# Attention's v product with seven block products in seven of sixteen units, and the probabilities' block moves at once over two queues

## Chip, cores and metric

The kernel runs on one core of a Trainium2 chip. The metric is the device time of one execution in microseconds; three runs of the kernel before gave 2028.94, 2030.40 and 2030.67 us, median 2030.40.

## What is computed

A two-layer decoder trunk in float32, 256 tokens of 2048 features: layer 0 mixes by causal pooling, layer 1 by attention with shared keys and values, and each has a gated convolutional feed-forward part after it. The part that matters here is layer 1's attention, 16 heads of 128 features:

```
k_shared = (h @ shared_w_k).reshape(B_, S, N_HEADS, HEAD_DIM)
v_shared = (h @ shared_w_v).reshape(B_, S, N_HEADS, HEAD_DIM)
...
q = (h @ w_q).reshape(B_, S, N_HEADS, HEAD_DIM)
for window, dil in DILATED_BRANCHES:
    o, lse = _dilated_branch(q, k, v, window, dil)
...
o = jnp.sum(wts[..., None] * jnp.stack(outs, axis=0), axis=0)
return o.reshape(B_, S, D_MODEL).astype(h.dtype) @ w_o
```

The three branches read the same scores with different masks, so the kernel merges them into one set of probabilities a head: exp of the masked scores, weighted by how many branches see a key.

## The kernel before

The program is a list of **units**. A unit is one 512x512 block of a weight (1 MB), its load, its split, its matmuls and, for the last block of a group, a `post` that takes the sums from PSUM. Float32 accuracy comes from splitting each weight and each activation in a high and a low part and adding three products. PE runs the units in the order of the list; `run_units` (from L130) does this for each unit i:

- `ahead(i)` (L111) issues loads up to five units ahead from SP's queue (L72) into three `raw` buffers, and splits up to three units ahead: ACT casts the high part (L82), DVE subtracts for the low part (L83), into four `wh` and four `wl` buffers;
- then the unit's matmuls on PE;
- then whatever was put off with `later(n, fn)` and is due now, n units after it was put off; then `post`.

An engine runs its instructions in the order in which this program writes them. So what `later` writes stands on DVE behind splits for units up to three further on, and a transfer on SP stands behind the loads written before it and ahead of those written after.

`group` (L165, L166: 16 pairs of a 128x512 and a 128x256 matmul) makes the feature-major products K, q and o-proj, with four PSUM accumulators of 128 features; `group_tm` (L238 to L240: 24 matmuls of 128x512) makes the token-major ones, such as v, with two. `group_tm` can also take units as **seven products**: the block is cut in 2x2, combinations of the quarters are made, and seven block products replace eight (L227 to L229, 42 matmuls of 128x256). Such a unit becomes two, "a" (18 matmuls, 3 products) and "b" (24, 4 products, no load of its own); its splits are `split_sums` (L89 to L109): for "a" ACT casts twice (L103) and DVE does L104, L106 twice, L107, L109; for "b" ACT casts twice (L96) and DVE subtracts twice (L97). The `raw` buffer of the block is free only when "b" is split. In the kernel before the feed-forward parts use this and attention doesn't.

Attention runs over four quarters hq of the output columns, four heads each: K(hq), q(hq), v(hq), four units each, then o-proj. For a quarter, put off from the end of q:

- `scores` for two heads at a time: PE L988, L989 into PSUM; DVE L994 to L1011 and ACT L1001 make probabilities, two heads in one tile `p`;
- `blocks` for quarters 0 to 2: DVE transposes 32x32 blocks within `p` (L1034) into a buffer `pb`, and 16 DMAs of 32 partitions by 6 runs of 128 bytes (L1043) put each block where the full transpose has it, tile `pTs`; all 16 on SP, eight after one unit and eight after two;
- `transposes` for quarter 3 instead: PE transposes, three a head (L1026), ACT copies;
- `outputs` for two heads: PE L1056, L1057 multiply by v (`vt`, from `v_post`, L952), ACT casts (L1058) and DVE subtracts (L1059) into `o`, which o-proj reads.

One buffer of its pool is left for `pb`, so the DVE transpose of a quarter's second pair of heads waits for all 16 moves of the first.

Of the kernel before, what the change touches and what calls it, by code (L numbers as in the profile page):

```python
# [9 lines left out]
F32 = mybir.dt.float32  # L10
F32R = mybir.dt.float32r
I32 = mybir.dt.int32
AF = mybir.ActivationFunctionType
OP = mybir.AluOpType
# [3 lines left out]
T = 256  # L18
P = 128
# [13 lines left out]
def trunk(ctx: ExitStack, tc: tile.TileContext, x, pool_w_in, pool_w_grp, pool_scale, pool_w_out,  # L33
          attn_w_q, attn_w_o, shared_w_k, shared_w_v, ffn_w_up, ffn_conv_w, ffn_conv_b, ffn_w_down,
          ln1_g, ln1_b, ln2_g, ln2_b, out):
    nc = tc.nc
    V, A, PE = nc.vector, nc.scalar, nc.tensor
# [7 lines left out]
    lnp = ctx.enter_context(tc.tile_pool(name="lnp", bufs=1))  # L45
    psp = ctx.enter_context(tc.tile_pool(name="psp", bufs=8, space=bass.MemoryType.PSUM))

    def bank(nm):
        return psp.tile([P, 512], F32, name=nm, tag="ps")
# [70 lines left out]
    def later(n, fn):  # L120
        if n == 0:
            fn()
        else:
            pending.append([n, fn])
# [52 lines left out]
    def group(w, r0s, c0, ncol, xqs, post, mode="ab", mids=(), shifted=False):  # L177
        ps = []
        for j, (r0, nr) in enumerate(r0s):
            last = j == len(r0s) - 1  # L180
            units.append((w[r0:r0 + nr, c0:c0 + ncol],
                          mm_quad(xqs[j], ps, j == 0, last, mode, mids[j] if j < len(mids) else None, shifted),
                          (lambda: post(ps)) if last else None))
# [98 lines left out]
    def quad_tile(nm):  # L282
        return xcp.tile([P, 4, 2, XW], F32R, name=nm, tag="xc")

    def lo_part(dst, src, n):
        V.tensor_tensor(dst[:, 0:n, 1, :T], src, dst[:, 0:n, 0, :T].bitcast(F32), OP.subtract)

    def split_act(dst, src):
        n = src.shape[1]
        A.copy(dst[:, 0:n, 0, :T], src)  # L290
        lo_part(dst, src, n)

    rows4 = [(512 * j, 512) for j in range(4)]

    pools = {}
    H, XC, XP, ST = {}, {}, {}, {}
    vec, cvec, gbx = [], [], {}
    ident = const.tile([P, P], F32, name="ident")
# [8 lines left out]
    xsrcs = [lambda j=j: XC[j] for j in range(4)]  # L307
# [150 lines left out]
    def add_last(w, rows, srcs, first, lay, which, after=None):  # L458
        for c in range(4):
            group(w, rows, 512 * c, 512, srcs, resid_last(c, first, lay, which, after),  # L460
                  mode="a" if c == 3 else "ab", shifted=c > 0 and not first)
# [481 lines left out]
    scale = 1.0 / math.sqrt(P)  # L943
    qk, pr, oq, pT, vts = {}, {}, {}, {}, {}

    def v_post(c):
        def post(t, ps):
            if t == 0:
                vts[c] = pools["attn"].tile([P, 2, 512], F32, name="vt", tag="vt")
                A.copy(vts[c][:, 0, :], ps)  # L950
            else:
                V.tensor_copy(vts[c][:, 1, :], ps)  # L952
                if c == 3:
                    later(1, lambda: transposes(c, (0, 1)))
                    later(2, lambda: transposes(c, (2, 3)))
                later(2 if c == 3 else 4, lambda: outputs(c, (0, 1)))
                later(3 if c == 3 else 7, lambda: outputs(c, (2, 3)))
        return post

    def qk_post(nm, hq):  # L960
        def post(ps):
            later(2 if hq == 0 and nm == "k" else 0, lambda: evac(ps))

        def evac(ps):
            ap = pools["attn"]
            o = ap.tile([P, 4, T], F32, name=nm, tag=nm)
            qk[nm] = o

            if hq == 0 and nm == "k":
                norm_evac(ps, 4, lambda m: o[:, m, :])  # L970
            else:
                for m in range(4):
                    A.copy(o[:, m, :], ps[m][:, T:])
                    V.tensor_tensor(o[:, m, :], o[:, m, :], ps[m][:, :T], OP.add)
            if nm == "q":
                later(2, lambda: scores(hq, range(0, 2)))
                later(3, lambda: scores(hq, range(2, 4)))
                if hq < 3:
                    later(4, lambda: blocks(hq, (0, 1)))
                    later(7, lambda: blocks(hq, (2, 3)))  # L980
        return post

    def scores(hq, ms):
        ap = pools["attn"]
        for m in ms:
            ps = bank("s")
            q, k = qk["q"][:, m, :], qk["k"][:, m, :]
            PE.matmul(ps[:, 0:P], q[:, :P], k[:, :P], start=True, stop=True)  # L988
            PE.matmul(ps[:, P:3 * P], q[:, P:], k, start=True, stop=True)  # L989
            if m % 2 == 0:  # L990
                two = ap.tile([P, 2, 3, P], F32, name="p", tag="p", bufs=2)
            s = two[:, m % 2]
            sf, nf, cf = (t.rearrange("p a b -> p (a b)") for t in (s, negm, cnt))
            V.scalar_tensor_tensor(sf, ps[:, :3 * P], scale, nf, op0=OP.mult, op1=OP.add)  # L994
            mx = ap.tile([P, 6], F32, name="mx", tag="mx", bufs=4)
            parts = ((0, slice(0, P)), (1, slice(P, 3 * P)))
            for t, sl in parts:
                V.tensor_reduce(mx[:, t:t + 1], sf[:, sl], AX.X, OP.max)
            V.tensor_scalar(mx[:, 2:4], mx[:, 0:2], -1.0, None, op0=OP.mult)
            for t, sl in parts:  # L1000
                A.activation(sf[:, sl], sf[:, sl], AF.Exp, bias=mx[:, 2 + t:3 + t])  # L1001
            pr[hq, m] = (s, mx, two)
        for m in ms:
            s, mx, _ = pr[hq, m]
            sf, cf = (t.rearrange("p a b -> p (a b)") for t in (s, cnt))
            for t, sl in parts:
                V.scalar_tensor_tensor(sf[:, sl], sf[:, sl], 1.0, cf[:, sl], op0=OP.mult, op1=OP.mult,
                                       accum_out=mx[:, 4 + t:5 + t])
            V.reciprocal(mx[:, 0:2], mx[:, 4:6])
            for t, sl in parts:  # L1010
                V.tensor_scalar(sf[:, sl], sf[:, sl], mx[:, t:t + 1], None, op0=OP.mult)  # L1011

    def turned(hq, ms):
        pool, tag = (pools["attn"], "pT") if ms[0] == 0 else (lnp, "sq")
        t = pool.tile([P, 2, 3 * P], F32, name="pTs", tag=tag)
        for m in ms:
            pT[hq, m] = t[:, m % 2]
        return t

    def transposes(hq, ms):  # L1020
        t = turned(hq, ms)
        for m in ms:
            ps = bank("pT")
            s = pr.pop((hq, m))[0]
            for i in range(3):
                PE.transpose(ps[:, i * P:(i + 1) * P], s[:, i, :], ident)  # L1026
            A.copy(t[:, m % 2], ps[:, :3 * P])


    def blocks(hq, ms):  # L1030
        two = pr.pop((hq, ms[0]))[2]
        pr.pop((hq, ms[1]))
        b = hp.tile([P, 6 * P], F32, name="pb", tag="h")
        V.transpose(b, two.rearrange("p h s k -> p (h s k)"))  # L1034

        t = turned(hq, ms)
        to = t.rearrange("p h s -> p (h s)").rearrange("p (k a j) -> p a k j", k=6, a=4)
        fr = b.rearrange("p (k b j) -> p b k j", k=6, b=4)

        def move(rows):  # L1040
            for i in rows:
                for j in range(4):
                    nc.sync.dma_start(to[32 * j:32 * j + 32, i], fr[32 * i:32 * i + 32, j])  # L1043

        later(1, lambda: move((0, 1)))
        later(2, lambda: move((2, 3)))

    def outputs(hq, ms):
        if ms[0] == 0:
            oq[hq] = quad_tile("o")  # L1050
        vt = vts[hq]
        for m in ms:
            hd = slice(m * P, (m + 1) * P)
            ps = bank("o")
            t = pT.pop((hq, m))
            PE.matmul(ps[:, :T], vt[:, 0, hd], t[:, :T], start=True, stop=False)  # L1056
            PE.matmul(ps[:, P:T], vt[:, 1, hd], t[:, T:], start=False, stop=True)  # L1057
            A.copy(oq[hq][:, m, 0, :T], ps[:, :T])  # L1058
            V.tensor_tensor(oq[hq][:, m, 1, :T], ps[:, :T], oq[hq][:, m, 0, :T].bitcast(F32), OP.subtract)  # L1059

    for hq in range(4):
        x0 = hq == 0
        group(shared_w_k, rows4, 512 * hq, 512, psrcs if x0 else xsrcs, qk_post("k", hq), mode="x" if x0 else "ab")
        group(attn_w_q[0], rows4, 512 * hq, 512, xsrcs, qk_post("q", hq))
        group_tm(shared_w_v, rows4, 512 * hq, 512, xsrcs, v_post(hq))
    add_last(attn_w_o[0], rows4, [lambda j=j: oq[j] for j in range(4)], True, 1, 0, after=to_tokens)
    marks.append(len(units))
    ffn(1)
# [141 lines left out]
```

## Time and profile before

| | before |
|---|---|
| median of three runs | 2030.40 us |
| profiled execution, its own time | 2030.49 us |
| its span in the profile | 2028.6 us |
| PE busy | 2021.7 us (100%), 12496 matmuls |
| DVE busy | 1674.5 us (83%) |
| ACT busy | 1257.2 us (62%) |
| POOL busy | 75.0 us (4%) |
| attention, start of K(0) to start of o-proj | 934.7 to 1218.3 us |

How to read what follows: a timeline row is start, duration, engine, line, operation, output<-inputs, shapes and count, and in brackets the idle time just before it with what ended it. A duration includes what overlaps with the next instruction of the engine, so the cost of a matmul or a DVE operation in a row of them is the distance between two starts. A group row has busy time and mean duration in nanoseconds. A DMA row ends with the median from issue to landing.

### The profile page before, as it was taken

Reading aid. Unit: us, or ns where it says so; the run is one execution under the profiler, and the core shown is the slowest. Engines: PE = TensorE matmul, PEld = TensorE weight load, DVE = VectorE, ACT = ScalarE, POOL = GpSimd, SP = SyncE. Lnnn points to the kernel's source line nnn. Section 1 sums busy time; section 2 is a strip of 40 time slices with the busy share of each in tenths; the row PEclk is TensorE's granted clock in tenths of the full one; section 3 lists DMA queues with packets and bytes.
Section 4 is the critical chain, followed back from the end, with each engine's and each line's share of the span. In section 5 each row is a group of like instructions: output and inputs, shape, how many; then the busy total and the mean of one; then the engine's idle time right before and its main releaser. Section 6 shows DMA issues by size and latency. Waiting matters only on the chain.

```text
span 2028.6 us, 31127 instructions
## 1 busy us (share of the span) xinstructions
PE 2021.7 (100%) x12496; PEld 1809.4 (89%) x12496; DVE 1674.5 (83%) x1998; ACT 1257.2 (62%) x1685; POOL 75.0 (4%) x111
## 2 busy tenths in 40 slices
PE   9999999999999999999999999999999999999999
PEld 8898988899889988889888888998899989989987
DVE  6859887899789999879756657787889888989898
ACT  5544686667766676657533444577667676667672
POOL 2000000000000001100000000000000000100100
PEclk9999999999999999999999999999999999999999
DMA  8565467666655757864566554557666756666665
GB/s 257 201 206 188 165 209 210 190 192 225 210 191 187 234 188 219 232 226 165 191 197 195 169 185 168 187 178 216 187 198 197 228 187 213 198 213 196 209 214 180
DMA packets 278305, 405.92 MB, mean 200 GB/s; under 512 B 80414, under 2 KB 95668, under 8 KB 277904
## 3 DMA queue, kind: packets, MB, share of 16 engines
q1 hardware_dynamic: 266144, 389.72, 57.9%
q0 software_dynamic: 11584, 13.55, 4.4%
q8 instruction: 98, 1.61, 0.3%
q10 hardware_dynamic: 432, 0.66, 0.1%
q14 instruction: 47, 0.39, 0.1%
HBM read 380.01 MB, written 2.10 MB: 188 GB/s over the span
## 4 chain that ended last, share of the span: by engine, by line
PE 99%; DMA 0%; SPq 0%; DVE 0%; ACT 0%; issue 0%; DVEq 0%
PE acc L165 43%; PE acc L166 22%; PE t L238 3%; PE t L239 3%; PE t L240 3%; PE acc L169 3%; PE acc L170 3%; PE acc L168 3%; PE s L228 3%; PE s L229 3%; PE s L227 3%; PE t L228 2%; PE t L227 2%; PE t L229 2%; PE s L989 0%; PE o L1056 0%
## 5 line engine op out<-in xcount | busy, mean ns | idle before, releaser
L165 PE MATMUL acc<-xc,wh 128*128 128x512 f32 x3264 | 1151.9, 396 | 0.0
L166 PE MATMUL acc<-xc,wl 128*128 128x256 f32 x3264 | 916.3, 281 | 0.0
L83 DVE TENSOR_TENSOR wl<-raw,wh 128x2048 fp32r<-128x2048 f32 (+2 forms) x320 | 692.4, 2168 | 248.4 <-ACT wh L82 243.9
L165 PEld LDWEIGHTS acc<-xc,wh 128*128 128x128 f32 x3264 | 616.0, 189 | 143.7 <-DVE o L1059 0.6
L82 ACT CAST wh<-raw 128x2048 fp32r<-128x2048 f32 (+2 forms) x320 | 578.1, 1812 | 225.7 <-PE acc L165 118.3
L166 PEld LDWEIGHTS acc<-xc,wl 128*128 128x128 f32 x3264 | 615.5, 189 | 0.5
L96 ACT CAST wh<-raw 128x1024 fp32r<-128x1024 f32 x112 | 117.4, 1053 | 150.2 <-DVE raw L107 134.1
L97 DVE TENSOR_TENSOR wl<-raw,wh 128x1024 fp32r<-128x1024 f32 x112 | 133.8, 1221 | 0.5 <-ACT wh L96 0.5
L103 ACT CAST wh<-raw 128x1024 fp32r<-128x1024 f32 x112 | 87.7, 832 | 41.2 <-PE acc L165 24.7
L106 DVE TENSOR_TENSOR wl<-raw,wh 128x1024 fp32r<-128x1024 f32 x112 | 101.9, 951 | 1.3 <-ACT wh L103 0.9
L586 ACT ACTIVATE c<-u,cv 128x256 f32<-128x256 f32 x172 | 89.5, 593 | 19.4 <-DVE f L649 8.2
L228 PE MATMUL t<-wl,g 128*128 128x256 f32 x328 | 92.2, 281 | 0.0
L227 PE MATMUL t<-wh,g 128*128 128x256 f32 x328 | 92.1, 281 | 0.0
L229 PE MATMUL t<-wh,g 128*128 128x256 f32 x328 | 91.9, 280 | 0.0
L271 POOL DMA_DIRECT2D ht<-w x24 | 20.3, 847 | 1808.1 <-ACT wh L103 1060.1
L577 ACT COPY u<-acc 128x256 f32<-128x256 f32 x164 | 54.0, 372 | 46.9 <-PE acc L166 46.8
L229 PE MATMUL s<-wh,xs 128*128 128x256 f32 x296 | 82.6, 279 | 0.0
L228 PE MATMUL s<-wl,xs 128*128 128x256 f32 x296 | 82.6, 279 | 0.0
L227 PE MATMUL s<-wh,xs 128*128 128x256 f32 x296 | 82.5, 279 | 0.0
L591 ACT ACTIVATE a<-u,cv 128x256 f32<-128x256 f32 x172 | 73.6, 500 | 12.3 <-DVE g L659 6.5
L591 ACT ACTIVATE u<-u,cv 128x256 f32<-128x256 f32 x172 | 73.5, 500 | 0.0
L109 DVE TENSOR_TENSOR raw<-raw 128x1024 f32<-128x1024 f32 x56 | 68.6, 1225 | 1.9
(279 smaller groups left out, 3444.8 us busy)
## 6 DMA issues: line engine op xcount, KB each, us to landing
raw<-in_ffn_w_up_dram SPq DMA_DIRECT2D x160, 1024.0 KB, 4.9
raw<-in_ffn_w_down_dram SPq DMA_DIRECT2D x80, 1024.0 KB, 5.1
raw<-in_pool_w_out_dram SPq DMA_DIRECT2D x16, 1024.0 KB, 5.0
raw<-in_shared_w_k_dram SPq DMA_DIRECT2D x16, 1024.0 KB, 5.1
raw<-in_attn_w_q_dram SPq DMA_DIRECT2D x16, 1024.0 KB, 5.3
raw<-in_shared_w_v_dram SPq DMA_DIRECT2D x16, 1024.0 KB, 5.9
raw<-in_attn_w_o_dram SPq DMA_DIRECT2D x16, 1024.0 KB, 5.0
raw<-in_pool_w_in_dram SPq DMA_DIRECT2D x12, 1024.0 KB, 5.6
```

Source lines behind the costliest of these rows:

```text
L82: A.copy(wh[i][:, s], r[:, s])
L83: V.tensor_tensor(wl[i][:, s], r[:, s], wh[i][:, s].bitcast(F32), OP.subtract)
L96: A.copy(h[:, :, n], r[:, :, n])
L97: V.tensor_tensor(l[:, :, n], r[:, :, n], h[:, :, n].bitcast(F32), OP.subtract)
L106: V.tensor_tensor(l[:, k, n], r[:, k, n], h[:, k, n].bitcast(F32), OP.subtract)
L165: PE.matmul(ps[m], h[:, k, c], q[:, k, :, :T], start=st, stop=False)
L166: PE.matmul(ps[m][:, :T], l[:, k, c], q[:, k, 0, :T], start=False, stop=sp and not shifted)
L227: PE.matmul(to, xh, h[:, k, n], start=opens and kk == 0, stop=False)
L228: PE.matmul(to, xh, l[:, k, n], start=False, stop=False)
L229: PE.matmul(to, xl, h[:, k, n], start=False, stop=ends and kk == 1)
L586: A.activation(c[:, m, :], u[:, m, 2:], AF.Identity, scale=cv[:, 2, j:j + 1], bias=cv[:, 3, j:j + 1])
L591: A.activation(to[:, m, :], u[:, m, i:i + T], AF.Copy, scale=cv[:, i, j:j + 1])
```

## The change

1. **Seven products for v.** `v_group` takes blocks 1 to 3 of quarters 1 and 2 and block 3 of quarter 3 as seven products (seven of sixteen units). They need sums of the activations' quarters, made once in `v_sums` for blocks 3, 1 and 2, put off from the end of q(0). Four PSUM results are added in `v_early` (five operations) and `v_post`.
2. **Order.** Quarters 0 and 3 run K, q, v as before; quarters 1 and 2 run K, v, q.
3. **Moves.** All four quarters use `blocks`; `transposes` is gone. All 16 moves of a pair of heads are issued after one unit, eight from SP and eight from POOL.
4. **Times.** `blocks` and `outputs` are put off by a table of four numbers a quarter, from the end of q, where before `outputs` were put off from the end of v.

DVE at the end of v(2) and the start of q(2), after the change. wl230 and wl231 are the splits of v(2)'s last block ("a" and "b"), wl232 to wl234 those of q(2)'s first three; L1096 is the evacuation of the outputs of quarter 1 (L1059 before), two heads in each pair of rows:

```order
L106 TENSOR_TENSOR wl230_10736<-raw230_10651,wh230_10735 128x2x256
L107 TENSOR_TENSOR raw230_10651<-raw230_10651 128x2x256
L109 TENSOR_TENSOR raw230_10651<-raw230_10651 128x4x256
L97 TENSOR_TENSOR wl231_10771<-raw230_10651,wh231_10770 128x4x256 x2
L83 TENSOR_TENSOR wl232_10797<-raw232_10733,wh232_10796 128x2048
L83 TENSOR_TENSOR wl233_10827<-raw233_10768,wh233_10826 128x2048
L1096 TENSOR_TENSOR o_10848<-o_10849,o_10848 128x256
L1096 TENSOR_TENSOR o_10848<-o_10854,o_10848 128x256
L83 TENSOR_TENSOR wl234_10862<-raw234_10794,wh234_10861 128x2048
L1096 TENSOR_TENSOR o_10848<-o_10889,o_10848 128x256
L1096 TENSOR_TENSOR o_10848<-o_10894,o_10848 128x256
```

The same outputs before, during K(2) and q(2) (wl224 to wl228 are splits of q(2) and v(2)):

```order
L83 TENSOR_TENSOR wl224_10478<-raw224_10388,wh224_10477 128x2048
L1059 TENSOR_TENSOR o_10513<-o_10514,o_10513 128x256
L1059 TENSOR_TENSOR o_10513<-o_10519,o_10513 128x256
L974 TENSOR_TENSOR k_10532<-k_10532,acc_10344 128x256
L974 TENSOR_TENSOR k_10532<-k_10532,acc_10345 128x256
L974 TENSOR_TENSOR k_10532<-k_10532,acc_10346 128x256
L974 TENSOR_TENSOR k_10532<-k_10532,acc_10347 128x256
L83 TENSOR_TENSOR wl225_10544<-raw225_10434,wh225_10543 128x2048
L83 TENSOR_TENSOR wl226_10594<-raw226_10475,wh226_10593 128x2048
L83 TENSOR_TENSOR wl227_10632<-raw227_10541,wh227_10631 128x2048
L1059 TENSOR_TENSOR o_10513<-o_10667,o_10513 128x256
L1059 TENSOR_TENSOR o_10513<-o_10672,o_10513 128x256
```

The outputs of quarter 1 have moved from among ordinary units, three splits apart, to right behind the seven-product units, one split apart. In the built program the four accumulators of q(2) take the four PSUM banks of these outputs: the first two are free after the first pair of L1096, the other two after the second pair.

SP's queue in the same place, after (raw230 is v(2)'s last block, raw232 to raw235 are q(2)'s; the moves are those of quarter 1's two pairs of heads):

```order
L72 DMA raw228_10511<-in_shared_w_v_dram 128x4x512
L1081 DMA pTs_10556<-pb_10554 32x6x32 x8
L72 DMA raw230_10651<-in_shared_w_v_dram 128x4x512
L1081 DMA pTs_10692<-pb_10690 32x6x32 x8
L72 DMA raw232_10733<-in_attn_w_q_dram 128x4x512
L72 DMA raw233_10768<-in_attn_w_q_dram 128x4x512
L72 DMA raw234_10794<-in_attn_w_q_dram 128x4x512
```

and before, quarter 1's moves among the loads of q(2) (raw224, raw225) and v(2) (raw226 to raw228):

```order
L1043 DMA pTs_10334<-pb_10332 32x6x32 x8
L72 DMA raw224_10388<-in_attn_w_q_dram 128x4x512
L1043 DMA pTs_10334<-pb_10332 32x6x32 x8
L72 DMA raw225_10434<-in_attn_w_q_dram 128x4x512
L72 DMA raw226_10475<-in_shared_w_v_dram 128x4x512
L1043 DMA pTs_10474<-pb_10472 32x6x32 x8
L72 DMA raw227_10541<-in_shared_w_v_dram 128x4x512
L1043 DMA pTs_10474<-pb_10472 32x6x32 x8
```

Sixteen moves on SP have become eight a pair of heads, and loads of q(2) stand behind the second eight. On POOL the other eight of each pair stand one behind another, 64 in all, with nothing between them.

The diff:

```diff
--- before.py
+++ after.py
@@ -943,19 +943,66 @@
     scale = 1.0 / math.sqrt(P)
     qk, pr, oq, pT, vts = {}, {}, {}, {}, {}
 
+    def v_tile(c):
+        if c not in vts:
+            vts[c] = pools["attn"].tile([P, 2, 512], F32, name="vt", tag="vt")
+        return vts[c][:, 0, :], vts[c][:, 1, :]
+
     def v_post(c):
         def post(t, ps):
-            if t == 0:
-                vts[c] = pools["attn"].tile([P, 2, 512], F32, name="vt", tag="vt")
-                A.copy(vts[c][:, 0, :], ps)
+            v = v_tile(c)[t]
+            if c > 0:
+                V.tensor_tensor(v, v, ps, OP.add)
+            elif t == 0:
+                A.copy(v, ps)
             else:
-                V.tensor_copy(vts[c][:, 1, :], ps)
-                if c == 3:
-                    later(1, lambda: transposes(c, (0, 1)))
-                    later(2, lambda: transposes(c, (2, 3)))
-                later(2 if c == 3 else 4, lambda: outputs(c, (0, 1)))
-                later(3 if c == 3 else 7, lambda: outputs(c, (2, 3)))
+                V.tensor_copy(v, ps)
         return post
+
+    def v_early(c):
+        def early(p16, p75):
+            v0, v1 = v_tile(c)
+            left, right = v0[:, :256], v0[:, 256:]
+            A.copy(left, p16[:, :256])
+            V.tensor_tensor(right, left, p16[:, 256:], OP.add)
+            V.tensor_tensor(v1[:, :256], right, p75[:, :256], OP.add)
+            V.tensor_tensor(right, right, p75[:, 256:], OP.add)
+            V.tensor_tensor(v1[:, 256:], v1[:, :256], p75[:, 256:], OP.add)
+        return early
+
+    vsums = {}
+
+    def v_sums(q, then):
+        ap = pools["attn"]
+        x = H[q]
+        a11, a12, a21, a22 = (x[:, k:k + 2, t * P:t * P + P] for k, t in ((0, 0), (2, 0), (0, 1), (2, 1)))
+        f = ap.tile([P, 4, T], F32, name="f", tag="k")
+        d = [f[:, i].rearrange("p (k t) -> p k t", k=2) for i in range(4)]
+        V.tensor_tensor(d[0], a21, a22, OP.add)
+        V.tensor_tensor(d[1], d[0], a11, OP.subtract)
+        V.tensor_tensor(d[2], a21, a11, OP.subtract)
+        V.tensor_tensor(d[3], a12, d[1], OP.subtract)
+
+        def rest():
+            if q < 3:
+                t = quad_tile("xsum")
+                vsums[q] = [[t[:, i, hl, :T].rearrange("p (k t) -> p k t", k=2) for hl in range(2)] for i in range(4)]
+                split_act(t, f)
+                then()
+                return
...
+            vsums[q] = [[u.rearrange("p (k t) -> p k t", k=2) for u in v] for v in vs]
+            then()
+
+        later(1, rest)
 
     def qk_post(nm, hq):
         def post(ps):
@@ -974,10 +1021,14 @@
                     V.tensor_tensor(o[:, m, :], o[:, m, :], ps[m][:, :T], OP.add)
             if nm == "q":
                 later(2, lambda: scores(hq, range(0, 2)))
+                b0, b1, o0, o1 = ((4, 7, 8, 11), (3, 5, 10, 11), (4, 7, 8, 11), (3, 5, 7, 8))[hq]
+                later(b0, lambda: blocks(hq, (0, 1)))
+                later(b1, lambda: blocks(hq, (2, 3)))
+                later(o0, lambda: outputs(hq, (0, 1)))
+                later(o1, lambda: outputs(hq, (2, 3)))
                 later(3, lambda: scores(hq, range(2, 4)))
-                if hq < 3:
-                    later(4, lambda: blocks(hq, (0, 1)))
-                    later(7, lambda: blocks(hq, (2, 3)))
+                if hq == 0:
+                    later(4, lambda: v_sums(3, lambda: v_sums(1, lambda: v_sums(2, lambda: None))))
         return post
 
     def scores(hq, ms):
@@ -1010,40 +1061,26 @@
             for t, sl in parts:
                 V.tensor_scalar(sf[:, sl], sf[:, sl], mx[:, t:t + 1], None, op0=OP.mult)
 
-    def turned(hq, ms):
-        pool, tag = (pools["attn"], "pT") if ms[0] == 0 else (lnp, "sq")
-        t = pool.tile([P, 2, 3 * P], F32, name="pTs", tag=tag)
-        for m in ms:
-            pT[hq, m] = t[:, m % 2]
-        return t
-
-    def transposes(hq, ms):
-        t = turned(hq, ms)
-        for m in ms:
-            ps = bank("pT")
-            s = pr.pop((hq, m))[0]
-            for i in range(3):
-                PE.transpose(ps[:, i * P:(i + 1) * P], s[:, i, :], ident)
-            A.copy(t[:, m % 2], ps[:, :3 * P])
-
-
     def blocks(hq, ms):
         two = pr.pop((hq, ms[0]))[2]
         pr.pop((hq, ms[1]))
         b = hp.tile([P, 6 * P], F32, name="pb", tag="h")
         V.transpose(b, two.rearrange("p h s k -> p (h s k)"))
 
-        t = turned(hq, ms)
+        pool, tag = (pools["attn"], "pT") if ms[0] == 0 else (lnp, "sq")
+        t = pool.tile([P, 2, 3 * P], F32, name="pTs", tag=tag)
+        for m in ms:
+            pT[hq, m] = t[:, m % 2]
         to = t.rearrange("p h s -> p (h s)").rearrange("p (k a j) -> p a k j", k=6, a=4)
         fr = b.rearrange("p (k b j) -> p b k j", k=6, b=4)
 
-        def move(rows):
-            for i in rows:
+        def move():
+            for i in range(4):
                 for j in range(4):
-                    nc.sync.dma_start(to[32 * j:32 * j + 32, i], fr[32 * i:32 * i + 32, j])
-
-        later(1, lambda: move((0, 1)))
-        later(2, lambda: move((2, 3)))
+                    by = nc.sync if i < 2 else nc.gpsimd
+                    by.dma_start(to[32 * j:32 * j + 32, i], fr[32 * i:32 * i + 32, j])
+
+        later(1, move)
 
     def outputs(hq, ms):
         if ms[0] == 0:
@@ -1058,11 +1095,20 @@
             A.copy(oq[hq][:, m, 0, :T], ps[:, :T])
             V.tensor_tensor(oq[hq][:, m, 1, :T], ps[:, :T], oq[hq][:, m, 0, :T].bitcast(F32), OP.subtract)
 
+    def v_group(hq):
+        js = (0, 1, 2, 3)
+        seven = {0: (), 1: (1, 2, 3), 2: (1, 2, 3), 3: (3,)}[hq]
+        group_tm(shared_w_v, rows4, 512 * hq, 512, xsrcs, v_post(hq),
+                 seven={j: (lambda j=j: vsums[j]) for j in js if j in seven}, early=v_early(hq))
+
     for hq in range(4):
         x0 = hq == 0
         group(shared_w_k, rows4, 512 * hq, 512, psrcs if x0 else xsrcs, qk_post("k", hq), mode="x" if x0 else "ab")
+        if hq in (1, 2):
+            v_group(hq)
         group(attn_w_q[0], rows4, 512 * hq, 512, xsrcs, qk_post("q", hq))
-        group_tm(shared_w_v, rows4, 512 * hq, 512, xsrcs, v_post(hq))
+        if hq in (0, 3):
+            v_group(hq)
     add_last(attn_w_o[0], rows4, [lambda j=j: oq[j] for j in range(4)], True, 1, 0, after=to_tokens)
     marks.append(len(units))
     ffn(1)
```

More of the change, by code (lines that the diff above doesn't have):

```diff
@@ new lines, in trunk @@
+    vsums = {}
[16 more added lines that the diff above has]
+                return
+            w = lnp.tile([P, 2, T], F32R, name="vs0", tag="fold2")
+            z = ap.tile([P, 2, T], F32R, name="vs3", tag="vs3")
+            vs = [[w[:, 0], w[:, 1]], [z[:, 0], z[:, 1]]]
+            for pair in (("S", "Q"), ("cs", "f1")):
+                vs.append([lnp.tile([P, T], F32R, name=f"vs{nm}", tag=nm) for nm in pair])
+            for i, v in enumerate(vs):
+                A.copy(v[0], f[:, i])
+            for i, v in enumerate(vs):
+                V.tensor_tensor(v[1], f[:, i], v[0].bitcast(F32), OP.subtract)
+            vsums[q] = [[u.rearrange("p (k t) -> p k t", k=2) for u in v] for v in vs]
+            then()
+        later(1, rest)
```

## The prediction

> **What bounds the kernel now.** I read first the page's busy times, the slices and the chain that ended last.
>
> ```profile
> span 2028.6 us, 31127 instructions
> ...
> PE 2021.7 (100%) x12496; PEld 1809.4 (89%) x12496; DVE 1674.5 (83%) x1998; ACT 1257.2 (62%) x1685; POOL 75.0 (4%) x111
> ...
> DVE  6859887899789999879756657787889888989898
> ...
> PE 99%; DMA 0%; SPq 0%; DVE 0%; ACT 0%; issue 0%; DVEq 0%
> ```
>
> PE is busy in the whole span and is 99% of the chain, so at first a microsecond of matmul taken away is a microsecond of time, and any wait that PE gets is time added. The 20th to 24th slices of DVE (fives, sixes, sevens; about 50.7 us each) are where attention lies. The same stretch cut into three windows:
>
> ```profile
> 934.00:1030.00 96.00, 96.00 (x560) 84.23 (x559) 75.58 (x102) 55.36 (x69) 0.00 (x0) 1.00 0.56 184
> 1030.00:1130.00 100.00, 100.00 (x529) 85.40 (x528) 57.48 (x82) 41.13 (x44) 0.00 (x0) 1.00 0.59 188
> 1130.00:1219.00 89.00, 89.00 (x461) 75.61 (x460) 58.11 (x118) 37.43 (x45) 0.00 (x0) 1.00 0.56 175
> ```
>
> The columns are length, PE, PEld, DVE, ACT, POOL, clock, DMA share and GB/s. PE has no gap in 285 us; DVE works 191 of them (67%), and POOL does nothing. The change spends DVE and POOL time there to take PE time away. The profiled execution took 2030.49 us, 1.9 beside its span and 0.1 above the median of 2030.40; I sum against 2030.5.
>
> **What PE saves.** One v unit now, and one seven-product unit as the feed-forward part has it:
>
> ```profile
> 1047.86 0.40 PE L238 MATMUL t<-wh,xc 128*128 128x512 f32 x1
> ...
> 1059.01 0.38 PE L988 MATMUL s<-k,q 128*128 128x128 f32 x2
> ...
> 1060.13 0.58 PE L238 MATMUL t<-wh,xc 128*128 128x512 f32 x1
> ```
>
> ```profile
> 1905.29 0.28 PE L227 MATMUL s<-wh,g 128*128 128x256 f32 x1
> ...
> 1910.23 0.28 PE L227 MATMUL s<-wh,g 128*128 128x256 f32 x1
> ```
>
> Two v units of 24 matmuls lie between the first pair: 11.15 us, 5.57 each; the scores pair behind them takes 1.1. The second fence has the first matmul of one seven-product unit and that of the next, 42 matmuls apart: 4.94 us (18 of them, 2.12, in its "a" half, 24, 2.83, in "b"). Seven units save 7 x 0.63 = 4.4 us. The transposes on PE go too:
>
> ```profile
> 1022.53 0.59 PE L1056 MATMUL o<-pTs,vt 128*128 128x256 f32 x2
> ...
> 1023.76 0.48 PE L165 MATMUL acc<-xc,wh 128*128 128x512 f32 x1
> ...
> 1223.95 0.82 PE L1026 MATMUL pT<-ident,p 128*128 128x128 f32 x6
> 1230.23 0.82 PE L1026 MATMUL pT<-ident,p 128*128 128x128 f32 x6
> 1230.89 0.38 PE L1056 MATMUL o<-pTs,vt 128*128 128x256 f32 x1
> ```
>
> An outputs pair takes 1.23. Six transposes took 0.66, both groups 1.3; of the 6.28 between their starts 5.62 are one unit of 32 matmuls, as in q, K and o-proj. PE is 5.7 us shorter: with no new wait the time would be 2024.8.
>
> **What DVE gets.** An ordinary split, a seven-product one, a scores pair and an evacuation of outputs:
>
> ```profile
> 1892.97 0.68 DVE L104 TENSOR_TENSOR raw<-raw 128x512 f32<-128x512 f32 x1
> ...
> 1897.30 2.41 DVE L97 TENSOR_TENSOR wl<-raw,wh 128x1024 fp32r<-128x1024 f32 x2
> 1899.63 0.68 DVE L104 TENSOR_TENSOR raw<-raw 128x512 f32<-128x512 f32 x1
> ```
>
> ```profile
> 1059.87 0.56 DVE L994 SCALAR_TENSOR_TENSOR p<-s,negm 128x384 f32<-128x384 f32 x1 [1.98 <-PE s L989]
> ...
> 1063.37 0.55 DVE L1011 TENSOR_SCALAR p<-p,mx 128x128 f32<-128x128 f32 x2
> ...
> 1065.25 2.29 DVE L83 TENSOR_TENSOR wl<-raw,wh 128x2048 fp32r<-128x2048 f32 x1
> 1067.46 0.55 DVE L994 SCALAR_TENSOR_TENSOR p<-s,negm 128x384 f32<-128x384 f32 x1
> ```
>
> ```profile
> 1024.44 0.42 DVE L1059 TENSOR_TENSOR o<-o 128x256 fp32r<-128x256 f32 x1 [0.23 <-ACT o L1058]
> 1024.79 1.40 DVE L974 TENSOR_TENSOR k<-k,acc 128x256 f32<-128x256 f32 x4
> 1090.65 0.98 DVE L1034 STREAM_TRANSPOSE pb<-p 128x768 f32<-128x768 f32 x1 [2.26 <-DMA pTs<-pb]
> ```
>
> From start to start: "a" 4.33, "b" 2.33, together 6.66 against 4.94 on PE and against 2.21 for an ordinary split (1065.25 to 1067.46); a scores pair 5.38; evacuations 0.42 each, four of K 1.40; the stream transpose 0.98. A chain of seven-product units on DVE thus runs slower than PE and lives on the lead that DVE had. The v sums in hq 0 (some 9 us of 512-wide adds and copies, by the 0.68 of L104) fall into K(1), whose four splits (8.8) and evacuations leave DVE over 5 us of margin; I count them, and v(1), at nothing. If that cover failed, the price would be what DVE is late, a few us.
>
> **The place that decides: v(2) into q(2).** Let 0 be the start of v(2)'s first unit (wh225) on PE. PE alone would run 5.57, then 1a to 7.7, 1b to 10.5, 2a 12.6, 2b 15.5, 3a 17.6, outputs (1.23) 18.8, 3b 21.7, outputs 22.9, then q(2). The scores of hq 1 follow q(1) and fall into K(2), two and one units before 0, so DVE starts on the first pair at -12.6 and from there has no gap: scores -7.2, split 1a -2.9, transpose -1.9, scores 3.5, 1b 5.8, K's evacuation 7.2, 2a 11.5, the second transpose 12.5 to 12.8, 2b 15.1, 3a 19.5, 3b 21.8. PE waits for its halves of 2b and 3b, 1.8 us in all, and asks for q(2) at 24.7. Its four accumulators are the banks that the outputs of hq 1 have just used, and the DVE order shows where those come free: behind the splits wl232 and wl233 for the first two, behind wl234 also for the other two. What those splits wait for:
>
> ```profile
> 1003.37 6.00 SPq L1043 DMA_DIRECT2D pTs<-pb  x8
> ...
> 1009.47 0.54 SPq L72 DMA_DIRECT2D raw<-in_attn_w_q_dram  x1
> ```
>
> ```profile
> raw<-in_attn_w_q_dram SPq DMA_DIRECT2D x16, 1024.0 KB, 5.3
> raw<-in_shared_w_v_dram SPq DMA_DIRECT2D x16, 1024.0 KB, 5.9
> ...
> pTs<-pb SPq DMA_DIRECT2D x96, 24.0 KB, 4.1
> ```
>
> ```profile
> 1048.33 1.92 ACT L82 CAST wh<-raw 128x2048 fp32r<-128x2048 f32 x1
> ```
>
> Eight moves hold SP for 6.0 us, 0.75 each. In the new order all eight of SP's half stand ahead of raw232's load, and they wait for the transpose: 12.8 + 6.0 = 18.8. raw232 lands at 24.1, is cast by 26.0, subtracted by 28.2; wl233 30.4; two evacuations 31.3; wl234, whose load had to wait until 3b was split (21.8 + 5.3 + 1.9 = 29.0, no bound any more), 33.5; the next evacuation 33.9. PE wants that third bank 0.7 after 24.7, so it stands **8.5 us**; with the 1.8 this place costs 10.3. Bounds: if all loads were early, DVE alone has three splits and three evacuations after 21.8, up to 29.7, a stall of 4.3 and 6.1 in all; if loads that overlap take the 5.9 of the v rows plus another's turn, some 3 more, 13. I take 10.3, the working by the medians. Nothing later gives it back, since PE has no idle time to fill.
>
> **The moves on POOL.** A move is 32 partitions by 6 pieces of 128 bytes, 192 pieces, which POOL has never issued in this trace. Its issues:
>
> ```profile
> 30.43 0.49 POOL L1119 DMA_DIRECT2D vrow<-in_pool_scale_dram  x1
> 30.91 1.89 POOL L1122 DMA_DIRECT2D crow<-in_ffn_conv_w_dram  x1
> ...
> 399.82 0.92 POOL L271 DMA_DIRECT2D ht<-w  x1 [316.24 <-ACT wh L103]
> 400.43 2.06 POOL L271 DMA_DIRECT2D ht<-u  x2
> ```
>
> 16 pieces took 0.49 and 258 took 1.89; a 128-partition issue 0.92, with the next one started 0.61 after it. The ends for t, the pace of a move on POOL, are 0.5 and 1.9, and 192 pieces lie as far from the row of 128 as from that of 258; I take the middle, 1.2. Where does t count? In hq 3 the second transpose waits on DVE for all 16 moves of the first pair, since one buffer holds pb. With 0 at the end of v(3)'s third unit on PE: first transpose done 3.8, its moves landed 3.8 + 7t + 4.1 (the last issue starts after seven others and lands 4.1 later, as from SP), DVE ready for the second at 13.7, its moves landed 1 + 7t + 4.1 after that. The outputs (3, 2-3) want them at 25.4: an outputs and a scores pair 2.3, v(3)'s last unit 4.94, three units of o-proj 16.9, outputs 1.2. Both rounds end to end are 13.0 + 14t, so up to t = 0.89 nothing is late; beyond it each 0.1 costs 1.4 us. At 1.2 that is **4.4 us**; at 0.5 nothing; at 1.9 it is 14, and some 4 more beside v(2), where the same wait pushes the chain above.
>
> The sum: 2030.5 - 5.7 + 10.3 + 4.4 = 2039.5.
>
> None of POOL's rows lies beside attention's DVE work. The Trainium skill, page "SBUF — State Buffer", section "SBUF: two separate sides", warns that a DMA issued from GpSimd has its descriptors written by GpSimd, which is shut out while a DVE instruction runs in a two-port mode. No run here shows it. In the stretch of the first pair's moves it could touch the scores' multiplications alone (two x two of 0.55 us in 5.38), so by that rule 1.1 us would be added to one round of moves and the sum would be 2040.6.
>
> Eight issues of 6.0 us against 4.1 to landing say that here issuing is the longer part. The Trainium skill, page "DMA: Bandwidth & Descriptors", section "Issuing engines are not separate DMA queues", says that several issuing engines save only the issue time, usually small beside the transfer. The trace agrees with the first half and not with "small"; by the page's "small" the second queue would bring nothing, and all 16 would be as late as from SP alone, 12 us, which is what t = 1.5 gives: 2043.7.
>
> **The rivals.**
> - *DVE is not late at q(2).* If the three splits did not stand ahead of the evacuations in time (loads early, and DVE's 34 us of work from -12.6 to 21.8 done some 8 us sooner, which is the point from which it decides), only the PE saving is left: 2024.8, or 2026.6 with the 1.8. For it speaks DVE's 67%; against it that those 34 us are a sum of measured rows without a gap. This is the other side: faster.
> - *POOL is quick (t under 0.89).* The hq 3 wait goes: 2030.5 - 5.7 + 10.3 = 2035.1; with the lower bound of the q(2) stall 2030.9, no change. For it speaks the 0.61 between two starts of 128-partition issues.
> - *POOL is slow.* The moves' six short runs per partition are priced like L1122's 258 pieces: t = 1.9, 2030.5 - 5.7 + 10.3 + 14 + 4 = 2053. Then the two queues don't do what they are said to do, as SP alone at 0.75 would be as quick.
> - *The saving is smaller,* as in a seven-product unit whose small matmuls wait for weight loads: at most the 4.4 of it, but the row of 4.94 was measured under the same conditions, so I give it nothing.
>
> **How the numbers follow.** Forecast (stall at q(2) of 8 to 13, t of 1.0 to 1.5): 2035 to 2046, 0.38. Quick POOL with the stall: 2031 to 2036, 0.32. DVE not late: 2024.8 to 2029 by t, 0.17. Slow POOL: 2046 to 2060, 0.13. A measurement tells 0.2%, 4.1 us, from no change: under 2026.3 is faster, over 2034.5 slower. Faster holds two thirds of the third case, 0.12; no change the rest of that and over half of the second, 0.25; slower 0.63. A range of 2026 to 2050 leaves out about 0.1 on each side.
>
> **What would show it.** Right: in the profile after, PE rows of L165 at the start of q(2) with idle time released by DVE o (the evacuation) or ACT wh, 6 to 12 us; PE idle before L1093 in hq 3, released by the DMA into pTs; POOL's issue rows near 1.2 each; PE's busy time lower by 5.7; a stream transpose waiting for pTs on DVE. Wrong: no PE gap over 1 us between 934 and 1219, or POOL rows under 0.9 with no wait in hq 3; or a gap elsewhere, at v(1) or at the sums, which I costed at nothing.

## The result and the profile after

The changed kernel takes 2036.52 us (median of 7 runs, 2034.85 to 2039.66) against 2030.40 (2028.82 to 2031.57): a ratio of 1.0033, 95% interval 1.0021 to 1.0044. It is 6.1 us slower. Its profiled execution took 2036.77 us with a span of 2034.7. The forecast was 2039.5 in a range of 2026 to 2050, slower.

The page after, its span, busy times, DVE's and the clock's slices and the chain:

```profile
span 2034.7 us, 31641 instructions
...
PE 2018.4 (99%) x12610; PEld 1811.6 (89%) x12610; DVE 1719.1 (84%) x2075; ACT 1270.3 (62%) x1708; POOL 111.5 (5%) x175
...
DVE  6859887899789999789887678787889888989899
...
PEclk9999999999999999999999899999999999999999
...
PE 97%; DVE 1%; DMA 1%; SPq 0%; issue 0%; ACT 0%; DVEq 0%; ACTq 0%
```

PE has lost 2% of the chain, to DVE and DMA, and one slice of the clock row, the 23rd, has an 8. That slice is 1119 to 1170 us. What PE waited for in the whole execution names the line:

```profile
PE acc L165 <- DVE o L1096: 8.4, 2, 7.2
PE acc L168 <- ACT wh L82: 1.8, 1, 1.8
PE warm L1139 <- DVE one L1135: 1.1, 1, 1.1
```

The columns are total, times and longest. The second and third belong to the program's start and were there before (1.6 and 1.1). The first is new: two waits, 7.2 and 1.3 us, of q(2)'s accumulators for the evacuation of quarter 1's outputs. They stand here on PE (the first row is v(2)'s first matmul, the L1093 and L1094 rows are the two pairs of outputs):

```profile
1093.46 0.40 PE L238 MATMUL t<-wh,xc 128*128 128x512 f32 x1
...
1112.36 0.39 PE L1094 MATMUL o<-pTs,vt 128*128 128x128 f32 x2
...
1115.71 0.59 PE L1093 MATMUL o<-pTs,vt 128*128 128x256 f32 x2
1116.14 0.38 PE L1094 MATMUL o<-pTs,vt 128*128 128x128 f32 x2
1116.36 0.60 PE L1093 MATMUL o<-pTs,vt 128*128 128x256 f32 x2
1116.80 0.39 PE L1094 MATMUL o<-pTs,vt 128*128 128x128 f32 x2
```

and then q(2)'s first matmuls:

```profile
1124.34 0.79 PE L165 MATMUL acc<-xc,wh 128*128 128x512 f32 x1 [7.16 <-DVE o L1096]
...
1127.27 0.80 PE L165 MATMUL acc<-xc,wh 128*128 128x512 f32 x1 [1.29 <-DVE o L1096]
...
1130.00 0.63 PE L165 MATMUL acc<-xc,wh 128*128 128x512 f32 x1
1130.43 0.35 PE L166 MATMUL acc<-xc,wl 128*128 128x256 f32 x1
1130.61 0.40 PE L165 MATMUL acc<-xc,wh 128*128 128x512 f32 x1
...
1130.97 0.39 PE L165 MATMUL acc<-xc,wh 128*128 128x512 f32 x1
```

A pair of matmuls takes 0.36 us from 1130.61 on, as always, and 0.61 just before. From 1124.34 to 1130.61 there are seven pairs in 6.27 us; less the 1.29 of waiting that is 4.98, where seven pairs at 0.36 are 2.5. So **the wait was followed by 2.5 us of slow matmuls**. The windows give the clock, in the last but two column:

```profile
1115.00:1120.00 5.00, 2.18 (x16) 1.88 (x14) 1.03 (x1) 2.17 (x2) 0.00 (x0) 1.00 1.05 397
1120.00:1125.00 5.00, 0.66 (x2) 0.57 (x3) 4.60 (x5) 4.51 (x7) 0.00 (x0) 0.53 0.86 274
1125.00:1130.00 5.00, 3.71 (x12) 2.82 (x11) 4.93 (x9) 2.28 (x3) 0.00 (x0) 0.50 0.99 374
```

The granted clock is half of full from 1120 to 1130. The Trainium skill, page "TensorE: Matmul & The Clock Gate", section "Part 1: The HAM clock gate (the "warmup" mystery)", says that PE's clock halves once PE has been idle for a window of about 3.4 us and returns after as long a busy one. The trace agrees: a half clock behind 7.16 us of idle time, and the full pace again at 1130.61, 3.3 us after the second wait ended.

What DVE, ACT and SP did before that:

```profile
1111.61 2.40 DVE L97 TENSOR_TENSOR wl<-raw,wh 128x1024 fp32r<-128x1024 f32 x2
1118.96 2.29 DVE L83 TENSOR_TENSOR wl<-raw,wh 128x2048 fp32r<-128x2048 f32 x1 [4.96 <-ACT wh L82]
1121.66 2.29 DVE L83 TENSOR_TENSOR wl<-raw,wh 128x2048 fp32r<-128x2048 f32 x1 [0.40 <-ACT wh L82]
1123.87 0.75 DVE L1096 TENSOR_TENSOR o<-o 128x256 fp32r<-128x256 f32 x2
1124.59 2.29 DVE L83 TENSOR_TENSOR wl<-raw,wh 128x2048 fp32r<-128x2048 f32 x1
```

```profile
1117.04 1.90 ACT L82 CAST wh<-raw 128x2048 fp32r<-128x2048 f32 x1 [4.29 <-DMA raw<-in_attn_w_q_dram]
1119.73 1.90 ACT L82 CAST wh<-raw 128x2048 fp32r<-128x2048 f32 x1 [0.79 <-DMA raw<-in_attn_w_q_dram]
1121.53 0.64 ACT L1095 CAST o<-o 128x256 fp32r<-128x256 f32 x2
```

```profile
1105.17 6.37 SPq L1081 DMA_DIRECT2D pTs<-pb  x8
1111.65 10.01 SPq L72 DMA_DIRECT2D raw<-in_attn_w_q_dram  x4
```

Read from the last fence upward: SP issues eight moves from 1105.17, so the load of raw232 goes out at 1111.65 and lands at 1117.04; ACT casts, and DVE, idle for 4.96 us, subtracts. Only behind the second such split come the evacuations. ACT's half of them, the casts of L1095, stands in the same way behind two casts of weights and starts at 1121.53. The first pair of outputs had been in PSUM since 1112.8, the second since 1117.2; both lay there while DVE first waited and then split weights that PE could not use yet for want of their banks.

POOL's own part was cheap:

```profile
L1081 POOL DMA_DIRECT2D pTs<-pb x64 | 36.5, 577 | 342.5 <-DVE f L982 145.8 <-PE acc L166 73.8 <-DVE k L1021 69.0
```

A move takes POOL 0.58 us, and no wait for pTs stands in PE's list.

### The profile page after: what moved, and what is told of

Read it like the earlier page. It is cut to its first block, busy times and chain, and to the rows that moved or that the text cites. A ratio compares the mean times of both kernels' runs of the same rounds, so it can differ in the third digit from the quotient of the medians.

```text
span 2034.7 us, 31641 instructions
## 1 busy us (share of the span) xinstructions
PE 2018.4 (99%) x12610; PEld 1811.6 (89%) x12610; DVE 1719.1 (84%) x2075; ACT 1270.3 (62%) x1708; POOL 111.5 (5%) x175
## 4 chain that ended last, share of the span: by engine, by line
PE 97%; DVE 1%; DMA 1%; SPq 0%; issue 0%; ACT 0%; DVEq 0%; ACTq 0%
PE acc L165 43%; PE acc L166 22%; PE acc L169 3%; PE acc L170 3%; PE acc L168 3%; PE s L228 3%; PE s L227 3%; PE s L229 3%; PE t L238 2%; PE t L240 2%; PE t L239 2%; PE t L228 2%; PE t L227 2%; PE t L229 2%; DMA raw<-in_attn_w_q_dram 0%; SPq L1081 0%
## 5 line engine op out<-in xcount | busy, mean ns | idle before, releaser
L83 DVE TENSOR_TENSOR wl<-raw,wh 128x2048 fp32r<-128x2048 f32 (+2 forms) x313 | 676.1, 2165 | 226.1 <-ACT wh L82 223.1
L82 ACT CAST wh<-raw 128x2048 fp32r<-128x2048 f32 (+2 forms) x313 | 564.6, 1809 | 218.2 <-PE acc L165 107.8
L96 ACT CAST wh<-raw 128x1024 fp32r<-128x1024 f32 x126 | 131.8, 1053 | 169.8 <-DVE raw L107 147.8
L97 DVE TENSOR_TENSOR wl<-raw,wh 128x1024 fp32r<-128x1024 f32 x126 | 150.3, 1220 | 1.0 <-ACT wh L96 1.0
L103 ACT CAST wh<-raw 128x1024 fp32r<-128x1024 f32 x126 | 98.7, 833 | 42.9 <-PE acc L165 24.6
L106 DVE TENSOR_TENSOR wl<-raw,wh 128x1024 fp32r<-128x1024 f32 x126 | 114.6, 950 | 2.3 <-ACT wh L103 2.1
L591 ACT ACTIVATE a<-u,cv 128x256 f32<-128x256 f32 x172 | 73.5, 499 | 12.3 <-DVE g L659 6.5
L109 DVE TENSOR_TENSOR raw<-raw 128x1024 f32<-128x1024 f32 x63 | 77.2, 1225 | 2.1
```

The lines of the kernel that those rows point to most:

```text
L82: A.copy(wh[i][:, s], r[:, s])
L83: V.tensor_tensor(wl[i][:, s], r[:, s], wh[i][:, s].bitcast(F32), OP.subtract)
L96: A.copy(h[:, :, n], r[:, :, n])
L97: V.tensor_tensor(l[:, :, n], r[:, :, n], h[:, :, n].bitcast(F32), OP.subtract)
L103: A.copy(h[:, k, n], r[:, k, n])
L106: V.tensor_tensor(l[:, k, n], r[:, k, n], h[:, k, n].bitcast(F32), OP.subtract)
```

## The experiments

**Theory A**: the evacuations of quarter 1's outputs stand on DVE behind splits whose weights are loaded late, because eight moves stand ahead of the load on SP; PE waits for the banks. **Theory B**: DVE simply has more work there than time (13 us of extra splits in v(2)). **C**: it is the moves that are late. **D**: the stall belongs to the new order or to the moves, not to the seven products. **E**: the issuing queue doesn't matter.

### Evacuations ahead of the splits

n is the number of units by which splits are written ahead, three without the added line; 229 to 231 are the last units of v(2), and 232 is the first of q(2).

```diff
         n = max(0, min(i - 1, SP_AHEAD) if i > 2 else 0)
+        n = {229: 2, 230: 1, 231: 1}.get(i, n)
```

> Changed kernel, but the splits wl232 to wl234 of q(2) are written up to two units later, so that the evacuations of quarter 1's outputs stand ahead of wl233 and wl234 on DVE. Theory A (the stall at q(2) is the wait for PSUM banks whose evacuations stand behind splits that wait for late loads): the third bank comes free after wl232 alone, some 5 us earlier; PE's idle time there falls from 8.45 us to about 4.5, in two or three pieces, and the time from 2036.5 to about 2032, or to 2030 if shorter pieces of idle time leave PE's clock alone. Theory B (DVE simply has too much work there): the work is the same, the idle time stays within 1 us of 8.45 and the time at 2036 to 2037.

Measured: 2030.61 us, ratio to before 1.0002 (0.9992 to 1.0011). PE's waits there (lines are one higher in this kernel):

```profile
PE acc L167 <- DVE wl L83: 1.8, 1, 1.8
...
PE acc L166 <- ACT wh L82: 1.4, 1, 1.4
```

The wait for the banks is gone. What is left is the wait for unit 232's own weights, first the high part, then the low one (3.2 us, less than the 4.5 expected; the two waits and the one matmul between them take 3.7). The same work in another order is worth 5.9 us, so A holds and B as the whole cause falls. The edit moves a split's ACT casts along with its DVE part, so the 5.9 us belong to the order on both engines. The clock is at 0.75 and 0.90 in the windows from 1120 to 1130, so a part of it was slow though the longer of the two waits was 1.8 us:

```profile
1120.00:1125.00 5.00, 3.32 (x13) 2.85 (x14) 4.93 (x10) 3.91 (x3) 0.00 (x0) 0.75 0.87 288
1125.00:1130.00 5.00, 5.00 (x28) 4.38 (x27) 5.00 (x4) 1.91 (x1) 0.00 (x0) 0.90 0.45 159
```

### The load ahead of the moves

```diff
-        later(1, move)
+        later(2 if (hq, ms[0]) == (1, 2) else 1, move)
```

> Changed kernel, but the 16 moves of quarter 1's second pair of heads are written one unit later, behind raw232's load on SP's queue instead of ahead of it. Theory A: raw232 is then early, the splits wl232 and wl233 end some 2.5 us sooner, and wl234's behind them; PE's idle time falls from 8.45 us to 5.5 to 6 and the time to about 2034. Theory B (DVE has too much work): DVE's 5 us of waiting for ACT at wl232 has no effect, no change. Rival C (the moves are what is late: outputs would wait for them): PE waits before L1093 and the time goes up.

Measured: 2033.41 us, ratio 1.0019 (1.0010 to 1.0027).

```profile
PE acc L165 <- DVE o L1096: 5.5, 2, 4.2
```

The wait shrinks from 8.4 to 5.5, at the lower end of what A expected, and stays the same kind of wait: raw232 is early now, but two splits still stand ahead of the evacuations. The interval overlaps that of the changed kernel (1.0021 to 1.0044), so the medians alone, 3.1 us apart, don't show that this edit helps; the shorter wait in the trace does. PE has no wait before L1093: C falls.

### Both

> Both edits: the load of raw232 ahead of the moves and the evacuations ahead of wl233 and wl234. Theory A: no bank and no load is late any more, PE's idle time at q(2) falls under 2 us and its clock stays at 1.00, so that the saving of 5.7 shows but for some 1 to 2 us: 2026 to 2027.5, faster than the kernel before. Theory B: as long as DVE's work is the bound, 2034 to 2037.

Measured: **2025.55 us, ratio 0.9977 (0.9967 to 0.9986)**, faster than the kernel before. In the same three windows PE has no gap and a full clock:

```profile
1115.00:1120.00 5.00, 5.00 (x29) 4.37 (x30) 4.93 (x9) 4.05 (x4) 0.00 (x0) 1.00 0.86 302
1120.00:1125.00 5.00, 5.00 (x30) 4.37 (x29) 4.93 (x3) 1.91 (x1) 0.00 (x0) 1.00 0.69 219
1125.00:1130.00 5.00, 5.00 (x31) 4.38 (x30) 2.29 (x1) 2.12 (x2) 0.00 (x0) 1.00 1.03 376
```

The time is 4.9 us below the kernel before, of the 5.7 that the matmuls save; it is half a microsecond under the expected range. DVE does all its work here. It was enough that nothing late stood ahead of what PE needed.

### Without seven products in v(2)

```diff
-        seven = {0: (), 1: (1, 2, 3), 2: (1, 2, 3), 3: (3,)}[hq]
+        seven = {0: (), 1: (1, 2, 3), 2: (), 3: (3,)}[hq]
...
-                b0, b1, o0, o1 = ((4, 7, 8, 11), (3, 5, 10, 11), (4, 7, 8, 11), (3, 5, 7, 8))[hq]
+                b0, b1, o0, o1 = ((4, 7, 8, 11), (3, 5, 7, 8), (4, 7, 8, 11), (3, 5, 7, 8))[hq]
```

(and v_post copies in quarter 2 instead of adding)

> Changed kernel, but the three seven-product units of v(2) are ordinary ones (four of sixteen stay); quarter 1's outputs are due after 7 and 8 units instead of 10 and 11, which is the same place beside v(2). The computation is the same. Theory A: without the late raw buffer and DVE's 13 us of extra splits there is no stall, the saving is 4 x 0.63 + 1.3 = 3.8: 2026.5 to 2027.5. Rival D (the stall belongs to the new order of v and q and to the moves, not to the seven products): a stall of 5 us or more stays at q(2), 2032 or above.

Measured: 2026.55 us, ratio 0.9982 (0.9973 to 0.9991). PE's list of waits has the program's start and one other, 0.6 us, far ahead of attention. D falls: with the same order and moves, the stall came with the three units of v(2). This run also takes DVE's extra work away, so it can't tell A from B; the runs above do. The rest of the change is worth the 3.8 us that its matmuls say.

### The moves and the order alone

All units of v ordinary, no sums, and the due numbers of outputs (and of quarter 3's second blocks) counted in fewer units:

```diff
-        seven = {0: (), 1: (1, 2, 3), 2: (1, 2, 3), 3: (3,)}[hq]
+        seven = ()
...
-                b0, b1, o0, o1 = ((4, 7, 8, 11), (3, 5, 10, 11), (4, 7, 8, 11), (3, 5, 7, 8))[hq]
+                b0, b1, o0, o1 = ((4, 7, 8, 10), (3, 5, 7, 8), (4, 7, 8, 11), (3, 4, 6, 7))[hq]
```

> Changed kernel without any seven-product unit in attention (no sums either); the new order, the block moves of all quarters over two queues stay, and outputs are due at the same places, counted in fewer units. The computation is the same. Theory A (the moves cost nothing, and the stall came from the seven-product units): only PE's transposes are saved, 2030.4 - 1.3 = 2029.1, within 1 us. Rival D (moves or order cost time by themselves): 2031 or above, with a PE wait for DVE o or for pTs.

Measured: 2028.52 us, ratio 0.9990 (0.9981 to 0.9999); PE has no wait in attention. That is 2.3 below the 2030.82 of the runs beside it and consistent with the 1.3 of the transposes; whether the rest is anything these runs can't tell.

### All moves from SP

```diff
-                    by = nc.sync if i < 2 else nc.gpsimd
+                    by = nc.sync
```

> Changed kernel with all 16 moves of a pair issued from SP. Theory A: 16 issues take some 12.5 us instead of 6.4 beside 4.6 on POOL; at v(2) the second transpose is some 3 us later and raw232's load 6 us more, PE's idle time there rises from 8.45 to 15 to 18 us; in quarter 3 the two rounds of moves end some 10 us after the outputs want them. Together 2050 to 2058. Rival E (a second issuing queue brings nothing, since all transfers share the same DMA engines): no change, 2036 to 2037.

Measured: 2052.27 us (4 runs, 2048.56 to 2053.95), ratio 1.0102 (1.0088 to 1.0116).

```profile
PE acc L165 <- DVE o L1096: 9.7, 2, 8.5
PE o L1093 <- issue: 4.7, 2, 4.1
PE o L1093 <- DMA pTs<-pb: 2.6, 1, 2.6
```

```profile
1090.80 10.33 SPq L1081 DMA_DIRECT2D pTs<-pb  x16
1104.86 11.71 SPq L1081 DMA_DIRECT2D pTs<-pb  x16
```

E falls: against eight on each queue, all sixteen on SP cost 15.7 us. Sixteen issues take 10.3 and 11.7 us, a little less than I gave them, and the waits are smaller than expected in both places (12.3 at v(2), 4.7 in quarter 3). The median lies in the expected range all the same, and the profiled execution, 2048.56, below it: the range was not met in the way that it was worked out. Some of the rest is slow clock, at 0.75 from 1113 to 1140 and 0.95 from 1235 to 1270 in the profiled execution (0.81 and 1.00 in the changed kernel).

### All moves from POOL

```diff
-                    by = nc.sync if i < 2 else nc.gpsimd
+                    by = nc.gpsimd
```

> Changed kernel with all 16 moves of a pair issued from POOL, 0.58 us each by the profile of the changed kernel, 9.3 for 16. Theory A: SP is free, so raw232's load is early and the stall at q(2) falls to 5 to 6 us as in the run with the late moves; in quarter 3 two rounds of 9.3 + 3.4 end some 4 to 5 us after the outputs want them, seen as a PE wait before L1093. Together 2036 to 2039: one wait in place of another. Rival E (the queue doesn't matter): 2036 to 2037 with the stall where it was, and no wait in quarter 3.

Measured: 2043.97 us (4 runs, 2041.18 to 2048.91), ratio 1.0072 (1.0055 to 1.0089). A miss, though of the kind foreseen:

```profile
PE o L1093 <- DMA pTs<-pb: 10.2, 2, 5.4
PE o L1093 <- issue: 1.6, 1, 1.6
```

The bank wait is gone altogether; raw232 comes early, and PE reaches the outputs late. One wait has taken the place of the other: the moves' own landing, 4.8 us beside v(2), where I had expected none of that, and 7.0 in quarter 3 (the 5.4 and the 1.6). POOL's queue shows that it stopped twice in the second round, so that these moves were later than 16 x 0.58:

```profile
1090.03 9.12 POOL L1081 DMA_DIRECT2D pTs<-pb  x16 [59.09 <-PE acc L166]
1105.10 6.21 POOL L1081 DMA_DIRECT2D pTs<-pb  x11 [5.95 <-PE t L229]
1112.25 0.57 POOL L1081 DMA_DIRECT2D pTs<-pb  x1 [0.94 <-DMA pTs<-pb]
1113.72 2.38 POOL L1081 DMA_DIRECT2D pTs<-pb  x4 [0.90 <-DMA pTs<-pb]
```

## Why the prediction held, and which terms were off

**The saving on PE, 5.7 us: right within the noise of the runs.** The run with both repairs is 4.9 under before, the one with four seven-product units 3.9 under it, where 3.8 was due. PE's busy time, which was to be lower by 5.7, is lower by 3.3; without the 2.5 us of slow matmuls it would be 5.8.

**The place and its chain: right, nearly to the microsecond.** With 0 at v(2)'s first matmul (1093.46), the prediction had raw232's load issued at 18.8 and landed at 24.1, its split done at 28.2, the first evacuations at 31.3, the third bank at 33.9. The rows above give 18.2, 23.6, 27.8, 31.1 and 33.8. Two small misses offset each other in part in the first of these: the moves were issued from 11.7, where 12.8 was given, and took 6.4, where 6.0 was given. The repairs show that each link matters: the order on DVE and ACT is worth 5.9 us, the order on SP 3.1, and both together 11.0.

**What PE lost there: 10.2 us where 10.3 was given.** Without any wait PE would have come to the third bank 23.6 after 0 (22.9 and the first two pairs of matmuls, 0.7); it came there at 33.8. The total is closer than its parts. Outputs ended at 1117.18, 23.7 after 0 against 22.9 without any wait, so the halves of 2b and 3b cost at most 0.8 where 1.8 was given. The rest went into the wait for the banks: 8.45 us of idle time (8.5 was given) and two pairs of matmuls at the slow clock between its two pieces.

**The clock: a term that the prediction didn't have.** Of the 2.5 us of slow matmuls 1.5 lie behind the third bank (five pairs in 3.34 us, where 1.8 is usual) and come on top. The other 1.0 lies between the two waits, where PE would have waited for the third bank anyhow.

**The moves on POOL: the mis-sized term.** I took 1.2 us a move, the middle between 0.5 and 1.9, "192 pieces lie as far from the row of 128 as from that of 258", and got 4.4 us of waiting in quarter 3. A move takes 0.58 and nothing waits there, neither PE before L1093 nor DVE's second transpose. This is one of the signs by which the prediction was to be wrong, POOL rows under 0.9 with no wait in quarter 3, and it came true for this term. The count of pieces was the wrong measure: 192 pieces of 128 bytes in 32 partitions take no longer than 128 pieces of 2 KB in 128 partitions, whose next issue started 0.61 later. The prediction had read that 0.61 and given it to the rival. What sets the time of an issue instead is not shown. The point from which the wait begins, 0.89, was not tested at that value; the run with all moves from POOL, two rounds of 16 x 0.58, does wait there, 7.0 us; by the prediction's own formula, with 15 x 0.58 in place of 7t, an estimate is 5.0.

The sum with the measured terms is 2030.5 - 5.7 + 10.2 + 1.5 = 2036.5. So of my rivals the quick POOL, 2035.1, came true with the clock on top. The point forecast of 2039.5 is 3 us high because a term of 4.4 that wasn't there stood in for one of 1.5 that I hadn't seen. That the time came out clearly on the slower side is partly luck: without the clock it would have been about 2035.0, half a microsecond above the 2034.5 from which the prediction counted it as slower.

The two other rules that I weighed: POOL's issues took 0.56 to 0.58 each whether DVE was in scores or in splits, so the lock of the Trainium skill's page "SBUF — State Buffer", section "SBUF: two separate sides", shows in none of these rows. By the Trainium skill's page "DMA: Bandwidth & Descriptors", section "Issuing engines are not separate DMA queues", the split over two queues saves only issue time, which is usually small. Here it was not small: it was worth 15.7 us of the kernel's time against all moves from SP and 7.5 against all from POOL.

## What to carry to other kernels

Where one engine is busy all the time, work moved to an idle engine is free only if nothing that the busy engine will need stands behind it in an in-order queue: look at what is *written behind* the added work, on the engine and on the DMA queue, and follow it to its latest operand. A share of 67% says nothing about that. The repair is then one of order, not of work: the same instructions took 11.0 us less with one group of transfers one unit later and three splits held back.

## What the runs showed of the hardware that I had not expected

- These PE waits cost more than themselves: 7.16 us of idle time were followed by a granted clock of 0.50 to 0.53 and 2.5 us of slow matmuls, 1.5 of them on top of the waiting. With the load ahead of the moves, waits of 4.2 and 1.3 us gave 0.50 in one window too. Two waits of 1.4 and 1.8 us, with one matmul between them, still gave 0.75 and 0.90.
- POOL's time for a DMA issue doesn't follow its pieces alone: 0.49 for 16, 0.58 for 192 short ones in 32 partitions, 0.92 for 128 long ones (0.61 from start to start), 1.89 for 258. These rows differ in partitions, in length and in where the data come from as well, so they don't tell what it does follow.
- POOL sometimes stopped issuing until an earlier move had landed. With all moves from POOL it did so nine times, 8.6 us in all; in the two rounds shown it went through 16 moves without a stop and then stopped after 11 and 12 of the next. In the changed kernel it did so once, for 0.26 us after seven moves. What sets this limit stays open.

```profile
who waited for it (us, times):
...
  POOL pTs L1081: 8.6, 9
```

```profile
1109.88 0.58 POOL L1081 DMA_DIRECT2D pTs<-pb  x1 [0.26 <-DMA pTs<-pb]
```
